# The last product of a mixer and the routing of 64 experts: other block widths, a fixed order on TensorE, and tables that move between pools

## The chip, the cores and the metric

The kernel runs on one core of one Trainium2 chip. The metric is the device time of one execution in microseconds (us); lower is better.

## What is computed

The reference runs two transformer blocks on 256 tokens of 1024 features, all in float32. The change lies at the seam between the second block's mixer and its mixture of experts:

```
merged = sigmoid(gc) * y_conv + sigmoid(ga) * y_attn
h = h + merged @ w_o                       # [256,1024] @ [1024,1024]
u = rmsnorm(h, norm2_g)
group = argmax(u @ w_group)                # 8 groups
two experts = the two highest of u @ w_router within that group (8 of 64)
y = sum over the two of weight * (silu(u @ w1[e]) * (u @ w3[e])) @ w2[e]
out = h + y
```

Each of the 64 experts has 6 MB of weights (w1, w3 of 1024 x 512, w2 of 512 x 1024), and the kernel reads all of them.

## The kernel before

**Stages.** The program runs the first block's mixer and feed-forward part, then the second block's projections, attention and convolution, then the gated merge (loop to L1052), the product with w_o (L1059 to L1086), the router (L1087 to L1205) and the expert loop (from L1290). VectorE, ScalarE, GpSimd and TensorE work on it under a scheduler that sets the order on each engine; the expert loop fixes TensorE's order by hand (`manual_schedule`).

**The product with w_o.** For full precision each weight tile is split into a high and a low part (`split`, L145 on ScalarE for the high part, L146 on VectorE for the low part), and three products are summed (`tokmm`, L269). Before the change the 1024 output columns are done in two blocks of 512. A block loads two tiles of 1 MB (L112), and each tile is split in two pieces, so there are eight pieces, 1 to 8. Each piece is used by 12 matmuls for token half t = 0 and 12 for t = 1. After a block VectorE adds the residual (L1067, result `h3`, which the program still calls xres), GpSimd writes a permuted copy `h3m` (L1070), TensorE turns h3 (L1077), ScalarE and VectorE scale it into `fT`, and TensorE forms the router's logits in `plg` (L1085).

**The router.** VectorE copies the logits to `lg` (L1088), finds the group (L1120 to L1124), masks the other groups (L1131, `rm`), takes the two best experts (L1134, L1136) and writes them as one-hot rows E1, E2 and their sum Eb in bf16 (L1142 to L1145). TensorE counts with Eb how many earlier tokens chose each expert (L1148 to L1150), VectorE makes the rank `rk` of each token (L1153, L1154) and a one-hot matrix `oh` (L1161, L1163), and TensorE gathers the tokens of four experts at a time with it (`gather`, L1171, evacuated at L1173). Then `up_mm` of expert 0 can start (L1238).

**The weights' queue.** SyncE (SP) issues the loads of expert weights, one tile of 1 MB each, in one fixed order (`load_exp`, issued at L758): tile 0, 1, 2, ... with six tiles per expert. Tile n goes to the slot that this string names, letter n modulo 21:

```
slot_order = "ggaccbbddddrrrrfeeeex"
...
p, tag, _ = slots[slot_order[n_exp[0] % len(slot_order)]]
...
with tc.issue_after(last[0]) if last else nullcontext():
    d = nc.sync.dma_start(dst, src)
```

So tiles 0 to 20 fill 21 slots, and tile 21 is the first that needs a slot again, the one of tile 0, after expert 0 has read it. `issue_after` keeps the order, and SP runs its instructions one after another: a load that waits holds up every load behind it. Tiles 0 to 4 are loaded during earlier stages. Tile 5 goes to the first buffer of pool b, tile 15 to pool f, tile 17 to a buffer of pool e.

**Where the slots lie.** The pools are laid out one after another in each partition of on-chip memory. `consts` comes first, then the ring (r), x and a, then the pools that the second block's mixer needs: `hla` (L126; eight buffers of 4096 bytes for the high and low pieces), `xpool` (L127) and others. When these are closed, the pools `small4`, `mo`, `wk4` and the slots f, b, d, e are laid into the same bytes, from where `hla` began. A tile of `pad` (L1102) lies between `wk4` and slot f:

```
pad = mo.tile([128, 80], F32, name="pad")
```

In the built program before the change `hla` ends at byte 106016 of the partition, `xpool` begins there, and so does the first buffer of pool b. A load into a slot waits until the last instruction that uses the bytes under it is done.

Of the kernel before, what the change touches and what calls it, by code (L numbers as in the profile page):

```python
# [9 lines left out]
F32 = mybir.dt.float32  # L10
# [86 lines left out]
def block_kernel(ctx: ExitStack, tc: tile.TileContext, A, out, dbg=None, stop=None):  # L97
# [7 lines left out]
    def dump(name, t):  # L105
        if name in dbg:
            nc.sync.dma_start(dbg[name], t)
# [74 lines left out]
    def cc(k):  # L182
        o, n = CLAY[k]
        return cst[:, o:o + n]
# [113 lines left out]
    def pc_(name="pc"):  # L298
        return psum.tile([128, 512], F32, name=name, tag="c", bufs=2)
# [756 lines left out]
    nc.scalar.dma_start(wr[:, :, 8:72], A["w_router_2"].rearrange("(k p) n -> p k n", p=128))  # L1056
    gain2 = pp("norm2")
    plg = pc_()
    for n in range(2):  # L1059
        pos = [pf(), pf()]  # L1060
        for pc in load_k(A["w_o_2"], n * 512, 512, "w_o"):
            for t in range(2):
                tokmm(pos[t], (mh, ml), t, [pc], first=(pc[0] == 0), last=(pc[0] == 6))
        for q in range(2):
            for t in range(2):
                c = slice(n * 512 + q * 256, n * 512 + (q + 1) * 256)
                nc.vector.tensor_add(h3[:, t, c], pos[t][:, q * 256:(q + 1) * 256], h2[:, t, c])  # L1067
        for t in range(2):
            p_ = slice(n * 64, (n + 1) * 64)
            nc.gpsimd.tensor_copy(h3m[:, t, :, p_], h3[:, t, n * 512:(n + 1) * 512].rearrange("q (p k) -> q k p", k=8))  # L1070

        for k2 in (2 * n, 2 * n + 1):
            pt = pt_()
            fT = wk.tile([128, 2, S], F32, name="fT", tag="sg", bufs=4)
            for k in range(2):
                for t in range(2):
# [5 lines left out]
            for k in range(2):  # L1082
                kt = 2 * k2 + k
                for t in range(2):
                    nc.tensor.matmul(plg[:, t * 72:(t + 1) * 72], fT[:, k, t * 128:(t + 1) * 128], wr[:, kt],  # L1085
                                     start=(kt == 0 and t == 0), stop=(kt == 7), skip_group_check=True)  # L1086
    lg = consts.tile([128, 2, 72], F32, name="lg")  # L1087
    nc.vector.tensor_copy(lg.rearrange("p t n -> p (t n)"), plg[:, :144])  # L1088
    small = consts
    rstd = rstd_of(h3, pc_(), "n4")  # L1090
    m3.close()
    dense.close()
    dump("h3", h3)
# [13 lines left out]
    def ps(name="ps"):  # L1107
        return psum.tile([128, 512], F32, name=name, tag="f", bufs=4)

    dump("lg", lg)  # L1110
    gainm = pp("norm2m")
    iota = cc("iota")
    io8 = iota[:, None, 0:8].to_broadcast([128, 2, 8])
    io64 = iota[:, None, 0:64].to_broadcast([128, 2, 64])

    gl8 = lg[:, :, 0:8]
    gm = small.tile([128, 2], F32, name="gm")
    goh = small.tile([128, 2, 8], F32, name="goh")
    gix = small.tile([128, 2], F32, name="gix")
    nc.vector.tensor_reduce(gm, gl8, axis=AX.X, op=OP.max)  # L1120
    nc.vector.tensor_tensor(goh, gl8, gm[:, :, None].to_broadcast([128, 2, 8]), op=OP.is_lt)
    nc.vector.scalar_tensor_tensor(goh, goh, 100.0, io8, op0=OP.mult, op1=OP.add)
    nc.vector.tensor_reduce(gix, goh, axis=AX.X, op=OP.min)
    nc.vector.tensor_tensor(goh, io8, gix[:, :, None].to_broadcast([128, 2, 8]), op=OP.not_equal)  # L1124
# [5 lines left out]
    for t in range(2):  # L1130
        nc.vector.scalar_tensor_tensor(rm[:, t].rearrange("p (g i) -> p g i", g=8), goh[:, t][:, :, None].to_broadcast([128, 8, 8]),  # L1131
                                       -3.0e38, lg[:, t, 8:72].rearrange("p (g i) -> p g i", g=8), op0=OP.mult, op1=OP.add)
# [9 lines left out]
    nc.vector.tensor_tensor(E1, io64, tif[:, :, 0:1].to_broadcast([128, 2, 64]), op=OP.is_equal)  # L1142
    nc.vector.tensor_tensor(E2, io64, tif[:, :, 1:2].to_broadcast([128, 2, 64]), op=OP.is_equal)
    nc.vector.tensor_add(Eb, E1, E2)
    nc.vector.tensor_add(Em, E1, E2)  # L1145

    pr = ps()
    nc.tensor.matmul(pr[:, 0:64], beforeb, Eb[:, 0], start=True, stop=True, skip_group_check=True)  # L1148
    nc.tensor.matmul(pr[:, 64:128], beforeb, Eb[:, 1], start=True, stop=False, skip_group_check=True)
    nc.tensor.matmul(pr[:, 64:128], onesb, Eb[:, 0], start=False, stop=True, skip_group_check=True)  # L1150
    rk = mo.tile([128, 2, 64], F32, name="rk")
    rk2, em2 = rk.rearrange("p t e -> p (t e)"), Em.rearrange("p t e -> p (t e)")
    nc.vector.scalar_tensor_tensor(rk2, pr[:, :128], 1.0, em2, op0=OP.add, op1=OP.mult)  # L1153
    nc.vector.tensor_scalar(rk2, rk2, -1.0, None, op0=OP.add)  # L1154
    io32 = iota[:, 0:32]

    def onehot(b4_):

# [7 lines left out]
    def gather(xg, oh, k4):  # L1166

        pg = ps()
        for k in range(4):
            for t in range(2):  # L1170
                nc.tensor.matmul(pg[:, k * 128:(k + 1) * 128], h3m[:, t, 4 * k4 + k],  # L1171
                                 oh[:, t].rearrange("p e s -> p (e s)"), start=(t == 0), stop=(t == 1))
        nc.vector.tensor_mul(xg[:, 4 * k4:4 * k4 + 4], pg.rearrange("p (k s) -> p k s", k=4),  # L1173
                             gainm[:, 4 * k4:4 * k4 + 4][:, :, None].to_broadcast([128, 4, 128]))

    by_group = {0: (wk.tile([128, 8, 128], F32, name="xg"), onehot(0))}
    gather(*by_group[0], 0)

    ge = small.tile([128, 2, 8], F32, name="ge")
    nc.vector.tensor_sub(ge, gl8, gm[:, :, None].to_broadcast([128, 2, 8]))  # L1180
# [17 lines left out]
    nc.tensor.matmul(pr[:, 128:192], onesb, Eb[:, 0], start=True, stop=False, skip_group_check=True)  # L1198
    nc.tensor.matmul(pr[:, 128:192], onesb, Eb[:, 1], start=False, stop=True, skip_group_check=True)
# [139 lines left out]
    with tc.If(most_r > SLOTS):  # L1339
# [6 lines left out]
        with tc.For_i(0, NE) as e:  # L1346
# [15 lines left out]
                                                   accum_out=dst[:, t:t + 1])  # L1362
            nc.vector.tensor_scalar(ecur, ecur, 1.0, None, op0=OP.add)
            for r in range(2):
                nc.vector.tensor_scalar(rke, rke, -float(SLOTS if r == 0 else 128), None, op0=OP.add)
# [73 lines left out]
```

## Time and profile before

| | |
|---|---|
| median of 3 runs | 1549.56 us (1547.82 to 1550.35) |
| the profiled execution's own time | 1547.5 us |
| its span, first to last instruction | 1545.7 us |
| TensorE's mean granted clock | 0.971 of full speed |
| busy: TensorE, VectorE, ScalarE, GpSimd | 88%, 39%, 27%, 8% of the span |
| read from HBM | 499.74 MB, 324 GB/s over the span |

Times in the views count from the span's start. "L758" is a line of the kernel. The 16 DMA engines are counted together: a DMA share of 1.00 means that all were moving data. Matmul ends are modelled, so neighbouring matmuls overlap in the rows, and a few matmul records can be missing.

### The profile page before, as it was taken

Reading aid. Unit: us, or ns where it says so; the run is one execution under the profiler, and the core shown is the slowest. Engines: PE = TensorE matmul, PEld = TensorE weight load, DVE = VectorE, ACT = ScalarE, POOL = GpSimd, SP = SyncE. Lnnn points to the kernel's source line nnn. Section 1 sums busy time; section 2 is a strip of 40 time slices with the busy share of each in tenths; the row PEclk is TensorE's granted clock in tenths of the full one; section 3 lists DMA queues with packets and bytes.
Section 4 is the critical chain, followed back from the end, with each engine's and each line's share of the span. In section 5 each row is a group of like instructions: output and inputs, shape, how many; then the busy total and the mean of one; then the engine's idle time right before and its main releaser. Section 6 shows DMA issues by size and latency. Waiting matters only on the chain.

```text
span 1545.7 us, 24722 instructions
## 1 busy us (share of the span) xinstructions
PE 1356.0 (88%) x10353; PEld 871.0 (56%) x10353; DVE 601.5 (39%) x1309; ACT 413.3 (27%) x734; POOL 126.8 (8%) x126
## 2 busy tenths in 40 slices
PE   7999999999999998999787888877787878878777
PEld 6766899998999996444343333333333433333332
DVE  5687777667876554322121221121111212211111
ACT  5455666555545442111000100000010100000011
POOL 3100132222111221000000000000000000000000
PEclk9999999999999999999999999999999999999999
DMA  9451656553546578999999999999999999999996
GB/s 321 131 180 56 220 190 230 176 181 107 190 140 217 190 252 341 418 419 419 419 419 419 419 419 419 419 419 419 419 419 419 419 419 419 419 419 419 419 419 243
DMA packets 137859, 502.43 MB, mean 325 GB/s; under 512 B 12545, under 2 KB 73490, under 8 KB 88722
## 3 DMA queue, kind: packets, MB, share of 16 engines
q1 hardware_dynamic: 134802, 499.67, 82.1%
q8 instruction: 83, 1.36, 0.4%
q10 hardware_dynamic: 2944, 1.16, 0.3%
q14 instruction: 30, 0.25, 0.0%
HBM read 499.74 MB, written 1.05 MB: 324 GB/s over the span
## 4 chain that ended last, share of the span: by engine, by line
DMA 56%; PE 38%; DVE 3%; SPq 1%; ACT 1%; issue 1%; POOL 0%; DVEq 0%; ACTq 0%
DMA w<-in_w 55%; PE pf L279 11%; PE pf L830 8%; PE pf L269 5%; PE acc L819 4%; PE oacc L1270 2%; PE ps L1238 2%; PE acc L269 1%; PE ps L1260 1%; PE ps L1171 1%; DMA w_go<-in_w_in 1%; DMA w_kv<-in_w_in 1%; PE pc L993 0%; PE pc L970 0%; PE pc L658 0%
## 5 line engine op out<-in xcount | busy, mean ns | idle before, releaser
L1238 PE MATMUL ps<-w,xg 128*32 128x256 f32 x4096 | 333.3, 416 | 158.8 <-DMA w<-in_w 156.4
L1238 PEld LDWEIGHTS ps<-w,xg 128*32 128x32 f32 x4096 | 145.8, 117 | 336.9 <-DMA w<-in_w 221.4
L1270 PE MATMUL oacc<-y,swT 128*128 128x512 f32 (+1 forms) x516 | 241.7, 611 | 0.6 <-DVE y L220 0.4
L1249 DVE TENSOR_TENSOR ar<-ps,a 64x128 f32<-64x128 f32 x128 | 48.9, 382 | 453.6 <-ACT a L1244 452.7
L1270 PEld LDWEIGHTS oacc<-y,swT 128*128 128x128 f32 x516 | 95.1, 195 | 128.2 <-issue 126.4
L1244 ACT ACTIVATE a<-ps 64x256 f32<-64x256 f32 x64 | 24.0, 375 | 516.0 <-PE ps L1238 516.0
L220 DVE COPY y<-ps 128x512 f32<-128x512 f32 x64 | 44.2, 691 | 218.3 <-PE ps L1260 218.3
L1260 PE MATMUL ps<-w,aT 128*32 128x512 f32 (+1 forms) x1032 | 124.5, 595 | 1.4 <-issue 1.4
L1222 ACT ACTIVATE swT<-ps 128x256 f32<-128x256 f32 x64 | 24.5, 383 | 215.7 <-PE ps L1220 215.5
L1171 PEld LDWEIGHTS ps<-oh,h3m 128*128 128x128 f32 x512 | 61.2, 196 | 26.7 <-issue 26.7
L1171 PE MATMUL ps<-oh,h3m 128*128 128x128 f32 x512 | 67.3, 286 | 1.0 <-DVE oh L1163 1.0
L218 ACT ACTIVATE y<-ps 128x512 f32<-128x512 f32 (+1 forms) x65 | 38.4, 590 | 110.1 <-PE ps L1260 110.0
L1260 PEld LDWEIGHTS ps<-w,aT 128*32 128x32 f32 x1032 | 27.4, 109 | 58.4 <-issue 46.5
L1173 DVE TENSOR_TENSOR xg<-ps,par 128x512 f32<-128x512 f32 x32 | 22.1, 691 | 69.9 <-PE ps L1171 69.9
L861 POOL TENSOR_TENSOR g<-uc,uc 128x256 f32<-128x256 f32 x22 | 31.7, 1439 | 160.1 <-ACT uc L859 151.4
L1213 DVE TENSOR_SCALAR sw<-cst,rk,Wm 128x128 f32<-128x128 f32 x128 | 38.1, 340 | 2.3 <-PE ps L1220 2.3
L1220 PEld LDWEIGHTS ps<-ident,sw 128*128 128x128 f32 x128 | 17.9, 142 | 33.9 <-issue 33.9
L146 DVE TENSOR_TENSOR w_downl<-w_down,w_downh 128x1024 fp32r<-128x1024 f32 x22 | 27.1, 1231 | 24.8 <-ACT w_downh L145 22.7
L819 PE MATMUL acc<-w_downh,gh 128*128 128x512 f32 x88 | 34.9, 397 | 0.0
L819 PE MATMUL acc<-w_downh,gl 128*128 128x512 f32 x88 | 34.8, 396 | 0.0
L819 PE MATMUL acc<-w_downl,gh 128*128 128x512 f32 x88 | 34.8, 395 | 0.0
L146 DVE TENSOR_TENSOR w_up1l<-w_up,w_up1h 128x1024 fp32r<-128x1024 f32 x22 | 26.9, 1221 | 17.1 <-ACT w_up1h L145 17.1
(532 smaller groups left out, 2179.3 us busy)
## 6 DMA issues: line engine op xcount, KB each, us to landing
w<-in_w SPq DMA_DIRECT2D x383, 1024.0 KB, 19.9
w_up<-in_w_up SPq DMA_DIRECT2D x22, 1024.0 KB, 5.2
w_down<-in_w_down SPq DMA_DIRECT2D x11, 1024.0 KB, 5.1
w_ccx<-in_w_in SPq DMA_DIRECT2D x8, 1024.0 KB, 5.0
w_g<-in_w_in SPq DMA_DIRECT2D x8, 1024.0 KB, 5.1
w_qkv<-in_w_in SPq DMA_DIRECT2D x6, 1024.0 KB, 5.1
w_out<-in_w_out SPq DMA_DIRECT2D x4, 1024.0 KB, 8.0
w_cb<-in_w_in SPq DMA_DIRECT2D x4, 1024.0 KB, 5.1
```

Source lines behind the costliest of these rows:

```text
L146: eng.tensor_sub(lo, src, hi.bitcast(F32))
L218: nc.scalar.activation(o, a, AF.Copy, scale=1.0 if scale is None else scale)
L220: nc.vector.tensor_copy(o, a)
L269: nc.tensor.matmul(o, xp[a][:, k0 + k, t * 128:(t + 1) * 128], wp[b][:, k], start=(first and j == 0 and n == 0), stop=(last and j == len(p ...
L279: nc.tensor.matmul(o, wp[b][:, k], xp[a][:, k], start=(n == 0), stop=(n == 23))
L819: nc.tensor.matmul(acc[2 * t + h], gp[a][:, t * 128:(t + 1) * 128], wd[b_][:, 0, h * 512:(h + 1) * 512], start=(ch == 0 and i == 0), stop= ...
L830: nc.tensor.matmul(pu[:, u * 256:(u + 1) * 256], cur[u][b_][:, k], hp[a][:, k], start=(kh == 0 and u == 0 and i == 0 and k == 0), stop=(i ...
L1171: nc.tensor.matmul(pg[:, k * 128:(k + 1) * 128], h3m[:, t, 4 * k4 + k], oh[:, t].rearrange("p e s -> p (e s)"), start=(t == 0), stop=(t == 1))
L1238: nc.tensor.matmul(ph[32 * g:32 * g + 32, 0:256].rearrange("p (q x) -> p q x", q=2), xg[:, 4 * k0 + k, 32 * i:32 * i + 32], w13[2 * k0 + u ...
L1249: nc.vector.tensor_mul(ar[64 * q:64 * q + 64].rearrange("p (r j) -> p j r", r=4), ph[64:128, s].rearrange("p (j r) -> p j r", r=4), a[64:1 ...
L1260: nc.tensor.matmul(py[32 * r:32 * r + 32, :n], aT[:, 32 * r:32 * r + 32], w(r), start=True, stop=True, tile_position=(0, 32 * r))
L1270: nc.tensor.matmul(oacc[2 * t + h][:, o:o + n], swT[:, t], y[:, :n], start=(e == 0), stop=(e == NE - 1), skip_group_check=True)
```

## The change

- The product with w_o is done in blocks of 512, 256 and 256 columns. The 256-column blocks load one tile of 1024 x 256 each. Pieces 5 and 6 now belong to the columns 512 to 767, pieces 7 and 8 to the columns 768 to 1023.
- TensorE's order here is written by hand: the transposes of a block stand inside the next block's second piece, before its t = 0 products, and the logits between t = 0 and t = 1. After the last block come two products of no use (`keep_busy`), the last transposes, three, the last logits, and ten; three more follow the rank products.
- VectorE no longer copies the logits (`lg` is now a view of `plg`), writes E1 and E2 in one step in bf16, no longer forms Eb, and no longer subtracts 1 from `rk` (the tables that it is compared with start at 1). The rank products read E1 and E2 in place of their sum.
- The first gather is done and evacuated in two halves.
- `gm`, `goh`, `gix`, `ge` and `rm` are now made from `consts`: the first four were in `small4`, `rm` shared a buffer in `wk4`. `lg` is gone from `consts`. `pad` is unchanged.

In bytes per partition: `consts` loses 576 (lg) and gains 512 (rm), 64 (goh), 64 (ge) and 32 each for gm and gix, in sum +128; `small4` loses 64 + 64 + 32 + 32 = 192. In the built program `hla` now ends at byte 106144, and the first buffer of pool b begins at byte 105952; slot f begins at 97760, and the `hla` buffer of the low part of piece 8 ends at 97952.

The diff, cut (the gather's halves, the exponent weights and the overflow path follow the same pattern):

```diff
-    for n in range(2):
+    PE = {mybir.EngineType.PE}
+
+    def keep_busy(n, o):
+
+        for _ in range(n):
+            nc.tensor.matmul(o.rearrange("p (r k) -> p r k", r=4), onesb, beforeb[:, None, :].to_broadcast([128, 4, 128]),
+                             start=True, stop=True, skip_group_check=True)
+
+    def block(c0, n, mids=()):
+
         pos = [pf(), pf()]
-        for pc in load_k(A["w_o_2"], n * 512, 512, "w_o"):
+        for i, pc in enumerate(load_k(A["w_o_2"], c0, n, "w_o")):
             for t in range(2):
-                tokmm(pos[t], (mh, ml), t, [pc], first=(pc[0] == 0), last=(pc[0] == 6))
+                if i == 1 and mids:
+                    mids[t]()
+                tokmm(pos[t][:, :n], (mh, ml), t, [pc], first=(pc[0] == 0), last=(pc[0] + pc[1][0].shape[1] == 8))
...
+    def turn(c0, n):
...
+    def logits(fTs):
...
+    with tc.manual_schedule(engines=PE):
+        block(0, 512)
+        fTs = []
+        for c0, n, c1, n1 in ((512, 256, 0, 512), (768, 256, 512, 256)):
+            block(c0, n, (lambda: fTs.append(turn(c1, n1)), lambda: logits(fTs[-1])))
+        idle = pf("idle")
+        keep_busy(2, idle)
+        f = turn(768, 256)
+        keep_busy(3, idle)
+        logits(f)
+        keep_busy(10, idle)
...
-    lg = consts.tile([128, 2, 72], F32, name="lg")
-    nc.vector.tensor_copy(lg.rearrange("p t n -> p (t n)"), plg[:, :144])
     small = consts
     rstd = rstd_of(h3, pc_(), "n4")
+
+    lg = plg[:, :144].rearrange("p (t n) -> p t n", t=2)
...
+    gm = small.tile([128, 2], F32, name="gm")
+    goh = small.tile([128, 2, 8], F32, name="goh")
+    gix = small.tile([128, 2], F32, name="gix")
+    rm = small.tile([128, 2, 64], F32, name="rm")
+    ge = small.tile([128, 2, 8], F32, name="ge")
...
-    gm = small.tile([128, 2], F32, name="gm")
-    goh = small.tile([128, 2, 8], F32, name="goh")
-    gix = small.tile([128, 2], F32, name="gix")
...
-    rm = wk.tile([128, 2, 64], F32, name="rm", tag="ar")
...
-    E12 = wk.tile([128, 2, 2, 64], F32, name="E12", tag="oh")
+    E12 = wk.tile([128, 2, 2, 64], BF, name="E12", tag="aT")
+    nc.vector.tensor_tensor(E12, io64, tif.rearrange("p t e -> p e t")[:, :, :, None].to_broadcast([128, 2, 2, 64]), op=OP.is_equal)
...
-    Eb = wk.tile([128, 2, 64], BF, name="Eb", tag="aT")
...
+    idle = ps("idle")
+    with tc.manual_schedule(engines=PE):
+        for i in range(2):
+            nc.tensor.matmul(pr[:, 0:128], beforeb, E12[:, i].rearrange("p t e -> p (t e)"), start=(i == 0), stop=False,
+                             skip_group_check=True)
+        for i in range(2):
+            nc.tensor.matmul(pr[:, 64:128], onesb, E12[:, i, 0], start=False, stop=(i == 1), skip_group_check=True)
+        keep_busy(3, idle)
...
-    nc.vector.tensor_scalar(rk2, rk2, -1.0, None, op0=OP.add)
-    io32 = iota[:, 0:32]
...
+    io32 = iota[:, 1:33]
...
-    gather(*by_group[0], 0)
...
+    gather(*by_group[0], 0, 2)
```

Two places of the order are needed below. The first is SP's list where the w_o tiles end and the expert tiles go on. In brackets stand the counters that an instruction waits for: DMAHW0 to DMAHW7 count landed loads, PE, DVE, Activation and Pool count finished work of TensorE, VectorE, ScalarE and GpSimd. Before the change, with tile 5 as w2_6565 and tile 6 as w1_2_6639:

```order
L112 DMA w_o_6240<-in_w_o_2 128x4x512 [waits DMAHW7_49,DVE_49]
L112 DMA w_o_6330<-in_w_o_2 128x4x512 [waits DMAHW0_49,DVE_49]
L758 DMA w2_6565<-in_w2_2 128x2048 [waits PE_49]
L112 DMA w_o_6340<-in_w_o_2 128x4x512 [waits DMAHW1_49,DVE_49]
L758 DMA w1_2_6639<-in_w1_2 128x2048
```

With the change, tile 5 is w2_6642, behind all four w_o tiles:

```order
L112 DMA w_o_6242<-in_w_o_2 128x4x512 [waits DMAHW7_49,DVE_49]
L112 DMA w_o_6308<-in_w_o_2 128x8x256 [waits DMAHW0_49,DVE_49]
L112 DMA w_o_6396<-in_w_o_2 128x8x256 [waits DMAHW1_49,DVE_49]
L758 DMA w2_6642<-in_w2_2 128x2048 [waits DVE_49,PE_49]
L758 DMA w1_2_6716<-in_w1_2 128x2048
```

Tile 5 has moved past the last w_o tile and waits for VectorE as well as for TensorE. In the built programs the counts mean this: before, TensorE's last product on w_g1l with xh (the first 8 KB of xpool); with the change, VectorE's split that writes w_ol_6311 and TensorE's last product that reads w_ol_6311, the low part of piece 5. Likewise tile 15 waited before for the last product on the low part of piece 7, and now waits for the last product on the low part of piece 8 (w_ol_6403).

The second place is TensorE's list from the end of the first 512 columns. Before (pt is a transpose, pc a logits product):

```order
L269 MATMUL pf_6229<-w_ol_6247,mh_5214 128x512 x2
L1077 MATMUL pt_6304<-ident_75,xres_67 128x128
L1077 MATMUL pt_6316<-ident_75,xres_67 128x128
L269 MATMUL pf_6328<-w_oh_6332,mh_5214 128x512 x2
L1077 MATMUL pt_6304<-ident_75,xres_67 128x128 x3
L1077 MATMUL pt_6316<-ident_75,xres_67 128x128 x3
L269 MATMUL pf_6328<-w_oh_6332,ml_5215 128x512 x2
```

With the change:

```order
L269 MATMUL pf_6231<-w_ol_6249,mh_5214 128x512 x2
L269 MATMUL pf_6306<-w_oh_6310,mh_5214 128x256 x4
L269 MATMUL pf_6306<-w_oh_6310,ml_5215 128x256 x4
L269 MATMUL pf_6306<-w_ol_6311,mh_5214 128x256 x4
L269 MATMUL pf_6307<-w_oh_6310,mh_5214 128x256 x4
L269 MATMUL pf_6307<-w_oh_6310,ml_5215 128x256 x4
L269 MATMUL pf_6307<-w_ol_6311,mh_5214 128x256 x4
L1091 MATMUL pt_6342<-ident_75,xres_67 128x128 x4
```

The 24 products of piece 5 now follow the first 512 columns directly, and the last row that names w_ol_6311 is the one that tile 5 waits for; the transposes come behind it.

## Rows read from the trace of the kernel before

**Rows 1.** The page's parts 1 and 4: the span and the chain that ended last.

```profile
span 1545.7 us, 24722 instructions
...
DMA 56%; PE 38%; DVE 3%; SPq 1%; ACT 1%; issue 1%; POOL 0%; DVEq 0%; ACTq 0%
```

**Rows 2.** Stretches: us, busy by engine, PEclk, DMA share, GB/s.

```profile
562.00:594.00 32.00, 32.00 (x199) 28.23 (x198) 15.78 (x18) 12.86 (x18) 8.52 (x7) 1.00 0.97 368
594.00:597.00 3.00, 3.00 (x15) 2.42 (x14) 0.00 (x0) 0.00 (x0) 0.00 (x0) 1.00 0.10 41
...
602.50:603.50 1.00, 0.18 (x2) 0.03 (x1) 0.78 (x7) 0.00 (x0) 0.00 (x0) 1.00 0.41 172
...
614.50:615.50 1.00, 1.00 (x11) 0.88 (x8) 0.00 (x0) 0.00 (x0) 0.00 (x0) 1.00 0.07 25
615.50:616.50 1.00, 1.00 (x11) 0.98 (x9) 0.00 (x0) 0.00 (x0) 0.00 (x0) 1.00 0.94 139
616.50:700.00 83.50, 81.36 (x738) 39.25 (x736) 23.42 (x64) 10.25 (x23) 0.00 (x0) 1.00 1.01 417
700.00:1530.00 830.00, 672.75 (x5450) 299.17 (x5450) 154.40 (x406) 75.51 (x168) 0.00 (x0) 0.95 1.01 417
```

**Rows 3.** SP's issues in order of time: start us, us, instruction; tiles 5, 6, 15, 17, 21.

```profile
562.31 0.34 SPq L758 DMA_DIRECT2D w<-in_w  x1
...
564.24 0.37 SPq L112 DMA_DIRECT2D w_o<-in_w_o  x1
564.66 0.50 SPq L758 DMA_DIRECT2D w<-in_w  x1
...
596.14 0.33 SPq L758 DMA_DIRECT2D w<-in_w  x1
...
602.75 2.03 SPq L758 DMA_DIRECT2D w<-in_w  x4
...
614.72 0.80 SPq L758 DMA_DIRECT2D w<-in_w  x2
```

**Rows 4.** The chain through 570 to 620 us: start us, us, what.

```profile
573.80 11.09 PE pf L269 x48
584.88 0.22 PE pt L1077 x2
...
598.94 0.43 DVE xres L1067
...
600.61 2.08 PE pc L1085 x16
602.69 0.02 issue
602.72 0.31 DVE lg L1088
...
607.17 0.13 DVE rk L1154
...
608.25 3.74 PE ps L1171 x16
...
612.76 1.93 PE ps L1238 x32
614.70 2.00 PE ps L1171 x16
```

**Rows 5.** The same chain earlier: 48 products of 256 columns, and eight transposes.

```profile
424.35 0.87 PE pt L985 x8
425.22 5.75 PE pf L279 x48
```

**Rows 6.** Stretches around the router: us, busy by engine, PEclk, DMA share, GB/s.

```profile
605.00:611.70 6.70, 4.05 (x21) 3.82 (x21) 4.55 (x28) 1.49 (x2) 0.00 (x0) 0.50 0.99 418
```

**Rows 7.** VectorE in order of time: a split of w_o, and the one-hot rows.

```profile
580.07 1.23 DVE L146 TENSOR_TENSOR w_ol<-w_o,w_oh 128x1024 fp32r<-128x1024 f32 x1 [1.56 <-ACT w_oh L145]
...
605.61 0.28 DVE L1143 TENSOR_TENSOR E<-cst,tif 128x128 f32<-128x128 f32 x1
```

**Rows 8.** The page's part 6: DMA issues, KB each, median us from issue to landing.

```profile
w_g<-in_w_in SPq DMA_DIRECT2D x8, 1024.0 KB, 5.1
w_qkv<-in_w_in SPq DMA_DIRECT2D x6, 1024.0 KB, 5.1
```

More of the change, by code (lines that the diff above doesn't have):

```diff
@@ L1058, in block_kernel @@
     plg = pc_()
[L1059 removed]
+    PE = {mybir.EngineType.PE}
[4 more added lines that the diff above has]
+    def block(c0, n, mids=()):
         pos = [pf(), pf()]
[L1061 removed]
+        for i, pc in enumerate(load_k(A["w_o_2"], c0, n, "w_o")):
             for t in range(2):
[L1063 to L1064 removed]
+                if i == 1 and mids:
+                    mids[t]()
+                tokmm(pos[t][:, :n], (mh, ml), t, [pc], first=(pc[0] == 0), last=(pc[0] + pc[1][0].shape[1] == 8))
+        for q in range(0, n, 256):
             for t in range(2):
[L1066 to L1067 removed]
+                c = slice(c0 + q, c0 + q + 256)
+                nc.vector.tensor_add(h3[:, t, c], pos[t][:, q:q + 256], h2[:, t, c])
         for t in range(2):
[L1069 to L1072 removed]
+            p_ = slice(c0 // 8, (c0 + n) // 8)
+            nc.gpsimd.tensor_copy(h3m[:, t, :, p_], h3[:, t, c0:c0 + n].rearrange("q (p k) -> q k p", k=8))
+    def turn(c0, n):
+        fTs = []
+        for k2 in range(c0 // 256, (c0 + n) // 256):
             pt = pt_()
             fT = wk.tile([128, 2, S], F32, name="fT", tag="sg", bufs=4)
[L1075 to L1076 removed]
+            for t in range(2):
+                for k in range(2):
                     nc.tensor.transpose(pt[:, k * 256 + t * 128:k * 256 + (t + 1) * 128],
@@ L1081, in block_kernel @@
                 copy(k, fT[:, k], pt[:, k * 256:(k + 1) * 256], scale=gain2[:, kt:kt + 1])
[L1082 to L1086, printed above, removed]
-    lg = consts.tile([128, 2, 72], F32, name="lg")
-    nc.vector.tensor_copy(lg.rearrange("p t n -> p (t n)"), plg[:, :144])
+                fTs.append((kt, fT[:, k]))
@@ new lines, in turn @@
+        return fTs
+    def logits(fTs):
+        for kt, fT in fTs:
+            for t in range(2):
+                nc.tensor.matmul(plg[:, t * 72:(t + 1) * 72], fT[:, t * 128:(t + 1) * 128], wr[:, kt],
+                                 start=(kt == 0 and t == 0), stop=(kt == 7), skip_group_check=True)
+    with tc.manual_schedule(engines=PE):
+        block(0, 512)
+        fTs = []
+        for c0, n, c1, n1 in ((512, 256, 0, 512), (768, 256, 512, 256)):
[6 more added lines that the diff above has]
+        keep_busy(10, idle)
@@ L1089, in block_kernel @@
     small = consts
     rstd = rstd_of(h3, pc_(), "n4")
+    lg = plg[:, :144].rearrange("p (t n) -> p t n", t=2)
+    iota = cc("iota")
+    io8 = iota[:, None, 0:8].to_broadcast([128, 2, 8])
+    io64 = iota[:, None, None, 0:64].to_broadcast([128, 2, 2, 64])
+    gl8 = lg[:, :, 0:8]
+    gm = small.tile([128, 2], F32, name="gm")
[3 more added lines that the diff above has]
+    ge = small.tile([128, 2, 8], F32, name="ge")
@@ new lines, in block_kernel @@
+    nc.vector.tensor_reduce(gm, gl8, axis=AX.X, op=OP.max)
+    nc.vector.tensor_tensor(goh, gl8, gm[:, :, None].to_broadcast([128, 2, 8]), op=OP.is_lt)
+    nc.vector.scalar_tensor_tensor(goh, goh, 100.0, io8, op0=OP.mult, op1=OP.add)
+    nc.vector.tensor_reduce(gix, goh, axis=AX.X, op=OP.min)
+    nc.vector.tensor_tensor(goh, io8, gix[:, :, None].to_broadcast([128, 2, 8]), op=OP.not_equal)
+    for t in range(2):
+        nc.vector.scalar_tensor_tensor(rm[:, t].rearrange("p (g i) -> p g i", g=8), goh[:, t][:, :, None].to_broadcast([128, 8, 8]),
+                                       -3.0e38, lg[:, t, 8:72].rearrange("p (g i) -> p g i", g=8), op0=OP.mult, op1=OP.add)
@@ L1091, in block_kernel @@
+    nc.vector.tensor_sub(ge, gl8, gm[:, :, None].to_broadcast([128, 2, 8]))
     m3.close()
@@ L1164, in onehot, with gather @@
         return oh
[L1166 to L1174, printed above, removed]
+    def gather(xg, oh, k4, n=4):
+        for k0 in range(4 * k4, 4 * k4 + 4, n):
+            pg = ps()
+            for k in range(n):
+                for t in range(2):
+                    nc.tensor.matmul(pg[:, k * 128:(k + 1) * 128], h3m[:, t, k0 + k],
+                                     oh[:, t].rearrange("p e s -> p (e s)"), start=(t == 0), stop=(t == 1))
+            nc.vector.tensor_mul(xg[:, k0:k0 + n], pg[:, :n * 128].rearrange("p (k s) -> p k s", k=n),
+                                 gainm[:, k0:k0 + n][:, :, None].to_broadcast([128, n, 128]))
     by_group = {0: (wk.tile([128, 8, 128], F32, name="xg"), onehot(0))}
-    gather(*by_group[0], 0)
-    ge = small.tile([128, 2, 8], F32, name="ge")
-    nc.vector.tensor_sub(ge, gl8, gm[:, :, None].to_broadcast([128, 2, 8]))
+    gather(*by_group[0], 0, 2)
     for t in range(2):
@@ L1197, in block_kernel @@
         nc.vector.scalar_tensor_tensor(Wm[:, t], E2[:, t], w2_[:, t:t + 1], Wm[:, t], op0=OP.mult, op1=OP.add)
-    nc.tensor.matmul(pr[:, 128:192], onesb, Eb[:, 0], start=True, stop=False, skip_group_check=True)
-    nc.tensor.matmul(pr[:, 128:192], onesb, Eb[:, 1], start=False, stop=True, skip_group_check=True)
+    for i in range(4):
+        nc.tensor.matmul(pr[:, 128:192], onesb, E12[:, i // 2, i % 2], start=(i == 0), stop=(i == 3), skip_group_check=True)
     most = mo.tile([128, 1], F32, name="most")
@@ L1364, in block_kernel @@
             for r in range(2):
-                nc.vector.tensor_scalar(rke, rke, -float(SLOTS if r == 0 else 128), None, op0=OP.add)
+                nc.vector.tensor_scalar(rke, rke, -float(SLOTS + 1 if r == 0 else 128), None, op0=OP.add)
                 so = wk.tile([128, 2, 128], F32, name="so", tag="oh")
```

23 lines of the change are left out of this document (2 added, 21 removed).

## The prediction

> **What bounds the kernel now.** I read the page first, then the stretches, then SP's issues, then the chain. The page says that transfers are 56% of the chain that ended last [rows 1]. The stretches say where: from 616.5 us to 1530 us the DMA share is 1.01 and the rate stays at 417 GB/s [rows 2]. For the last 900 us the kernel is a stream of 1 MB weight tiles that never stops, and TensorE, busy 672.75 of 830 us in the main stretch, keeps pace with it. One tile takes 1.0486 MB / 417 GB/s = 2.515 us. So the end is fixed by the moment from which the stream runs without a gap: every microsecond that this moment moves, the end moves.
>
> In the trace this moment is tile 21. Ahead of it the DMA engines are idle three times: at 594 to 597 (share 0.10), at 602.5 to 603.5 (0.41) and at 614.5 to 615.5 (0.07), about 2.7 + 0.6 + 0.9 = 4.2 us [rows 2]. Each gap ends with an issue by SP that had to wait: tile 15 at 596.14, tile 17 at 602.75, tile 21 at 614.72 [rows 3]. Tile 17 comes right behind the last logits (602.69), tile 21 right behind the first half of expert 0's products (612.76 + 1.93 = 614.69) [rows 4]. That is what the router's chain is worth: the gap before tile 21 is 0.9 us, and no more than the 4.2 us of all three can be won here, whatever the chain saves. A measurement of this kernel can tell about 0.2%, 3.1 us, from no change.
>
> **The layout.** This is the part of the change that its edits do not speak of, and I price it first. `consts` grows by 128 bytes and `small4` shrinks by 192, while `pad` stays. So, measured from `hla`, the slots f, b, d and e lie 192 bytes lower than before: the first buffer of pool b no longer begins where `xpool` does, but covers the last 192 bytes of `hla`'s last buffer (105952 to 106144). That buffer holds the low part of piece 5. SP's list shows the result: tile 5 now waits for VectorE too, and its counts stand for the split that writes w_ol_6311 and the last product that reads it.
>
> When is that? The first 512 columns start at 573.80 and take 11.09 us, so they end at 584.88 [rows 4]; nothing before them changes. Then come the 24 products of piece 5. 48 products of 256 columns took 5.75 us [rows 5], so 24 take 2.88: 587.76, and with a few hundredths for the release tile 5 is issued at **587.8**, where it was 562.31 [rows 3]. VectorE's split is done long before: its row starts at 580.07 and takes 1.23 us [rows 7]. The nearest other price for a product of 256 columns is the full one of 512 (11.09 / 48 = 0.231 us, 5.5 us for 24), which gives 590.4; the lower is half of it (0.116 us, 2.8 us), 587.7. I take 5.75 / 48, the same shape.
>
> SP works in order, so tiles 6 to 20, which before left from 564.66 on, stand behind tile 5. The last w_o tile still leaves at 564.24 (its wait is the same), lands some 5.1 us later [rows 8], and then the DMA engines have nothing until 588.7: a gap of 19 us under full work of TensorE. From there 16 tiles (5 to 20) need 16 x 2.515 = 40.2 us. So the stream reaches tile 21 as if it had been issued at 587.8 + 40.2 = 628.0, where it was 614.72. **The sum is +13.3 us.** It is less than the delay of tile 5, 25.5 us, because the old stream lost the difference itself: in its three gaps and by a rate of 368 GB/s at 562 to 594 [rows 2].
>
> **Does another wait come later still?** The product with w_o ends at 584.88 + 2 x 5.75 for the 256-column blocks + 0.87 + 2.08 for eight transposes and eight logits products (16 passes) + half of that again, 0.44 + 1.04, that now stand inside the blocks: 600.8, where it was 598.92 [rows 4, 5]. Tile 15, by the same shift of 192 bytes, waits for this end. The stream comes to it at 588.7 + 10 x 2.515 = 613.8, so that wait is covered, and so is tile 17's, for the last logits. They end 3.77 us after the last product before; half of the transposes and logits are gone from that stretch, so 3.77 - 0.44 - 1.04 = 2.3 us remain: 603.1, against 618.8 when tile 17's turn comes.
>
> **The router's parts,** which have to be reckoned for the rivals:
> - the copy of the logits, 0.31 us, goes, and the subtraction, 0.13 on the chain [rows 4]; three one-hot steps become one of double width, which saves between one and two of 0.28 us [rows 7]: together 0.7 to 1.0 us.
> - the idle products: the ten run while TensorE waits for VectorE anyway, the five before them cover the adds and the copies. I cost them at nothing; if their cover falls short by one product, that is 0.2 us, the price of a 512-column product.
> [...]
>
> [...] The stream reaches tile 21 only at 628.9. [...]
>
> [...]
>
> **The rivals.**
> - *A, not slower: tile 5's wait is met early,* say by an earlier user of the buffer, or the overlap does not count. It decides if tile 5 leaves before 614.72 - 40.2 = 574.5. Then tile 15 is next: 600.8 in place of 596.14, and six tiles later, 600.8 + 15.1 = 615.9, comes tile 21: +1.2 us, 1550.8. For it: before, tile 5 did not wait for w_o at all, and the overlap is 192 of 8192 bytes. Against it: the counter of VectorE is new in SP's list, and in the trace of before each of these issues follows its wait at once [rows 3, 4].
> - *B, the router decides:* both loads leave as they did, and the edits do what they add up to. Then tile 17 is the last wait, 603.1 + 4 x 2.515 = 613.2: -1.5 us, 1548.0; with all gaps gone 1545.4. For it speaks the clock at 0.50 in the gather; against it that the wait of tile 5 lies before all of it. [...]
> - *C, nothing is made up:* after the restart the stream stops again at tiles 15, 17 and 21, and the delay of 25.5 us stays whole: 1575.1. [...]
>
> **How the numbers follow.** The profiled execution took 1547.5 us with a span of 1545.7. With 13.3 us more, 1560.8 and 1559.0. The median of the runs, 1549.56, lies 2.1 us above that execution, so I expect a median of 1562.8, 0.86% more. Chances: 0.88 for this, 0.06 for A, 0.03 for B, 0.03 for C. The likely case alone spans 1560.8 less 1.3 us (the scatter of the runs) to 1565.5 (the dear price of piece 5's products) with as much above it; A, B and C hold little enough to be left outside: 1559.5 to 1566.5. Slower by over 0.2%: 0.88 + 0.03. Within 0.2%: A and most of B, 0.08. Faster: what is left of B, 0.01.
>
> **What would show it.** In the profile of the changed kernel SP should wait about 23 us, from 564.6 to 587.8, for TensorE on the w_o line; the DMA share should be near zero from some 569.5 to 588.7, and then 1.0 without a break to the end. Tile 21 should be issued by about 613 without starting a gap. The granted clock should be 1.00 through the first gather, and expert 0 should start some 2 to 3 us earlier than it did. I am wrong if tile 5 leaves before 577 us, or if the stream breaks again after 589.

## The result, and the profile after

The changed kernel takes **1559.38 us** (median of four runs, 1559.33 to 1559.99), the kernel before 1548.74 us on the same chip: ratio **1.0068**, 95% interval 1.0056 to 1.008, some 10.6 us slower. The sum had said 13.3 us. The profiled execution took 1559.99 us with a span of 1558.2 us; it starts its first expert tile 0.7 us later than the trace of before (160.54 against 159.81 us), so 0.7 us is taken off wherever the two are compared by time.

The page: the share of transfers in the chain that ended last is 62%, where it was 56% [rows 1].

```profile
span 1558.2 us, 24857 instructions
...
DMA 62%; PE 32%; DVE 3%; SPq 1%; ACT 1%; issue 0%; POOL 0%; DVEq 0%; ACTq 0%
```

What SP waited for from 560 to 640 us (total us, times, longest us):

```profile
SPq L758 <- DMA w<-in_w: 39.0, 19, 3.5
SPq L758 <- DVE w_ol L146: 13.9, 1, 13.9
SPq L758 <- PE pf L269: 10.3, 2, 9.2
```

The second row and the longest wait of the third are one wait, that of tile 5: for the split that writes the low part of piece 5, and then for the products that read it, 13.9 + 9.2 = 23.1 us (a forecast of 23). The third row's other wait, 1.1 us, is tile 15's, for the end of the product with w_o. The first row is new in this stretch: behind tile 5, SP waits 19 times for earlier loads, where before did so once here, for 0.5 us (and then 341 times from 640 to 1500 us). The chain below shows the pattern: tile 13 leaves at 593.58, and when it has landed, 21.23 us later, tile 21 follows at 614.88, eight tiles on. SP's issues (start us, us) and the chain (start us, us, what):

```profile
564.95 0.37 SPq L112 DMA_DIRECT2D w_o<-in_w_o  x1
588.47 26.74 SPq L758 DMA_DIRECT2D w<-in_w  x17
```

```profile
559.98 14.52 PE pf L279 x121
574.50 13.95 PE pf L269 x72
588.45 0.02 issue
588.47 5.05 DMA w<-in_w
...
593.58 21.23 DMA w<-in_w
...
614.88 20.07 DMA w<-in_w
```

Tile 5 leaves at 588.47 us, where before it left at 562.31 [rows 3]. It follows straight behind 72 products: 48 of the first 512 columns and the 24 of piece 5 (11.09 + 2.86 us). Less 0.7 us that is 587.8, the forecast. In before the chain ran through TensorE and the router to 616 us [rows 4]; now it turns to transfers at 588 and stays there. The stretches (us, busy by engine, PEclk, DMA share, GB/s):

```profile
569.50:588.50 19.00, 19.00 (x117) 16.91 (x116) 11.82 (x13) 7.09 (x8) 7.25 (x6) 1.00 0.01 1
588.50:589.50 1.00, 1.00 (x11) 1.00 (x10) 0.59 (x2) 0.07 (x1) 0.32 (x1) 1.00 0.21 41
589.50:600.00 10.50, 10.50 (x93) 10.50 (x92) 2.09 (x5) 3.37 (x9) 2.02 (x3) 1.00 1.00 392
600.00:603.00 3.00, 3.00 (x22) 2.05 (x20) 1.31 (x5) 1.17 (x3) 0.65 (x1) 1.00 1.01 421
605.00:612.00 7.00, 5.57 (x64) 3.63 (x61) 5.84 (x37) 1.98 (x4) 0.00 (x0) 1.00 1.02 421
616.50:700.00 83.50, 79.50 (x712) 38.80 (x705) 21.41 (x57) 9.87 (x22) 0.00 (x0) 1.00 1.01 419
700.00:1530.00 830.00, 670.01 (x5367) 296.45 (x5366) 152.09 (x400) 74.54 (x165) 0.00 (x0) 0.95 1.01 420
700.00:1500.00 800.00, 645.75 (x5184) 286.62 (x5183) 147.53 (x388) 71.83 (x159) 0.00 (x0) 0.95 1.01 420
```

Against [rows 2]: the three small gaps at 594, 602.5 and 614.5 us are gone, and one of 19 us stands in their place, with the DMA engines at 0.01. The last two rows hold a number that I had not priced, the rate: 420 GB/s. The 417 that before had up to 1530 us [rows 2] takes in the end of its stream (311 GB/s from 1515 to 1530 us), so the fair comparison is 700 to 1500 us: 420 against 419 (the row of before stands in experiment 4). In the router the granted clock is 1.00 at 605 to 612 us, where it was 0.50 [rows 6], and the rows of TensorE there show it:

```profile
603.58 2.32 PE L1064 MATMUL idle<-beforeb,onesb 128*128 128x512 bf16 x10
...
608.44 2.02 PE L1203 MATMUL ps<-oh,h3m 128*128 128x128 f32 x16 [0.54 <-DVE oh L1194]
610.39 1.93 PE L1268 MATMUL ps<-w,xg 128*32 128x256 f32 x32
```

The gather takes 2.02 us instead of 3.74 [rows 4]; expert 0 starts at 610.39 us, with the later start taken off 3.1 us earlier than before, and its first half ends at 612.3, some 2.6 us ahead of tile 21's issue at 614.88. So the router is faster as forecast, and it is worth nothing here (experiment 3 tests that).

### The profile page after: what moved, and what is told of

Read it like the earlier page. It is cut to its first block, busy times and chain, and to the rows that moved or that the text cites. A ratio compares the mean times of both kernels' runs of the same rounds, so it can differ in the third digit from the quotient of the medians.

```text
span 1558.2 us, 24857 instructions
## 1 busy us (share of the span) xinstructions
PE 1364.0 (88%) x10422; PEld 875.0 (56%) x10422; DVE 601.5 (39%) x1306; ACT 413.4 (27%) x734; POOL 127.2 (8%) x128
## 4 chain that ended last, share of the span: by engine, by line
DMA 62%; PE 32%; DVE 3%; SPq 1%; ACT 1%; issue 0%; POOL 0%; DVEq 0%; ACTq 0%
DMA w<-in_w 61%; PE pf L279 10%; PE pf L830 8%; PE pf L269 4%; PE acc L819 4%; PE acc L269 1%; DMA w_go<-in_w_in 1%; DMA w_kv<-in_w_in 1%; PE oacc L1300 0%; PE pc L993 0%; PE pc L970 0%; PE pc L658 0%; DVE tb L501 0%; PE pt L632 0%; SPq L330 0%
## 5 line engine op out<-in xcount | busy, mean ns | idle before, releaser
L1268 PE MATMUL ps<-w,xg 128*32 128x256 f32 x4096 | 337.1, 416 | 165.3 <-DMA w<-in_w 164.4
L1205 DVE TENSOR_TENSOR xg<-ps,par 128x512 f32<-128x512 f32 (+1 forms) x33 | 22.3, 675 | 67.0 <-PE ps L1203 67.0
```

The costliest lines, as they stand in the source:

```text
L1268: nc.tensor.matmul(ph[32 * g:32 * g + 32, 0:256].rearrange("p (q x) -> p q x", q=2), xg[:, 4 * k0 + k, 32 * i:32 * i + 32], w13[2 * k0 + u ...
```

## The experiments

Beside medians and ratios one number is read from each trace: the time from the landing of tile 26 to that of tile 382, 356 tiles of the unbroken stream. It repeated to 0.1 us between two profiles of one kernel (896.8 and 896.9 us before, 895.6 twice with the change), so it tells small steps that medians hide. A ratio is always to the kernel before on the same chip.

**1. The kernel before, twice, and the changed kernel again.** No edit.

> The kernel before, unchanged, as a measure of how far equal programs scatter and of how fast its stream of tiles runs in one more trace. If the missing 2.7 us of the prediction are scatter of the runs of before (S1), the ratio is 1.000 and the time from the landing of tile 26 to that of tile 382 differs from the 896.8 us of the first trace by about as much as the changed kernel's 895.6 does. If the stream really runs faster with the slots 192 bytes lower (S2), it is 896.8 again within 0.3.

> The changed kernel, unchanged, in five rounds. S1 (scatter of the few runs of before): 12 to 13 us above the kernel before in these rounds. S2 (a faster stream with the slots lower): 10 to 11 us again, and 895.6 us within 0.3 from the landing of tile 26 to that of tile 382.

Measured: before against itself 0.9997 (0.9988 to 1.0006), the changed kernel 1559.32 us, 1.0072 (1.0059 to 1.0086). The stream took 896.9 and 895.6 us again, so S2 holds: the stream of the changed kernel is 1.2 us shorter, and that is not scatter between traces. The medians lie 10.2 us apart, as S2 said. The profiled execution of before, 1549.78 us, is the slowest of its eleven runs here (the fastest took 1547.24). Its chain (start us, us, what), and TensorE's clock there, the first trace of before in the last row:

```profile
612.59 3.64 PE ps L1238 x32
616.23 2.58 PE ps L1171 x16
```

```profile
612.50:616.50 4.00, 3.91 (x33) 1.72 (x34) 0.03 (x1) 0.00 (x0) 0.00 (x0) 0.50 0.45 188
```

```profile
612.50:616.50 4.00, 3.74 (x48) 2.80 (x48) 0.21 (x1) 0.00 (x0) 0.00 (x0) 1.00 0.72 236
```

Expert 0's first half took 3.64 us at a granted clock of 0.50, where the first trace had 1.93 us [rows 4] with the clock back at 1.00. Tile 21 was issued at 616.26 instead of 614.72, and tile 26 landed 2.2 us later (635.72 against 633.48). So these two executions of before differ by 2 us (spans 1545.7 and 1547.9) through the moment at which the clock rises again after the router.

**2. The layout put right in the changed kernel; the layout alone in the kernel before.**

```diff
-    pad = mo.tile([128, 80], F32, name="pad")
+    pad = mo.tile([128, 128], F32, name="pad")     (in the changed kernel)
-    pad = mo.tile([128, 80], F32, name="pad")
+    pad = mo.tile([128, 32], F32, name="pad")      (in the kernel before)
```

> The changed kernel with pad enlarged by 48 floats (192 bytes), so that slots f and b lie again where they lay before, measured from hla; nothing else. Theory (the layout alone costs the time): tile 5 is issued at about 562 to 563 us again, the last wait that breaks the stream is tile 17's at about 603 us, and the kernel takes 1.5 us less than the kernel before (1 to 2.5 us less). Rival (the edits themselves cost the time, the 256-column blocks or the order by hand): still 10 us or more above the kernel before.

> The kernel before with pad made smaller by 48 floats (192 bytes), so that slots f, b, d and e lie as low as with the change; none of its edits. Theory (the layout alone): tile 5 waits for the last product on the low part of piece 5, which ended at about 590.3 us in the trace of before, so 590.3 + 40.2 - 614.7 = 15.8 us more by the sum of the prediction, and 13 to 16 us more if the medians fall short as they did with the change. Rival (the edits): no change within 1 us.

Measured: 1542.84 us, ratio **0.9964** (0.995 to 0.9977), and 1561.5 us, **1.0081** (1.0067 to 1.0095). The first of the two, the changed kernel with the pad of 128 floats, is called the good layout from here on. In it tile 5 leaves at 562 us again:

```profile
562.06 0.34 SPq L758 DMA_DIRECT2D w<-in_w  x1
564.00 0.37 SPq L112 DMA_DIRECT2D w_o<-in_w_o  x1
564.42 47.79 SPq L758 DMA_DIRECT2D w<-in_w  x17
```

SP's waits in the second, the old code with its slots 192 bytes lower:

```profile
SPq L758 <- DMA w<-in_w: 37.1, 18, 3.1
SPq L758 <- DVE w_ol L146: 13.9, 1, 13.9
SPq L758 <- PE pf L269: 11.9, 1, 11.9
```

and its stretch 570 to 590 us:

```profile
570.00:590.00 20.00, 20.00 (x116) 17.02 (x115) 11.89 (x15) 9.09 (x14) 7.54 (x6) 1.00 0.01 1
```

The same wait and the same hole, without one edit of the arithmetic: 192 bytes of overlap make the loss. But neither size fits. The shift alone cost 12.4 us where the sum said 15.8, and the changed kernel without it gained 5.6 us where I had 1.5. The traces say where to look. Up to the landing of tile 26 both sums hold: against the first trace of before, with the first expert tile's start taken off, the shift alone brings it 15.8 us later (649.78 against 633.48 us, less 0.5) and the good layout 1.6 us earlier (631.65, with 0.2 for an earlier start). What differs is the stream behind it: 896.8 and 896.9 us in the two profiles of before, 895.6 in both of the changed kernel, 893.9 and 894.2 here. The pace, which the prediction took as fixed, differs from program to program.

**3. Without the idle products, and another order of slots.**

```diff
-        for _ in range(n):
+        for _ in range(0):
```

```diff
-    slot_order = "ggaccbbddddrrrrfeeeex"
+    slot_order = "ggaccbbddddrrrrfexeee"
```

> The changed kernel with the pad of 128 floats and without the idle products in the router. Theory: the idle products only keep the clock up for the gather (2.02 us for its 16 products instead of 3.74 us before), and in this layout the tile that waits for expert 0's first half (issued 611.4 us with the idle products) is what the stream waits for. So it is issued 1.7 us later and the run ends 1 to 1.7 us later than with the pad alone: 1543.8 to 1544.6 us, ratio to before 0.997 to 0.9975. Rival: the load of that tile lands 7.7 us after its issue, against 5.1 us for a load that finds the engines free, so the queue is still full there and a delay of 1.7 us is hidden: 1542.8 us, the same as with the pad alone.

> The changed kernel as it is, without the idle products. Theory: the stream starts so late here (tile 5 issued 588.5 us) that the router has slack: a gather that is 1.7 us slower delays nothing, 1559.4 us, ratio 1.0065 to 1.0075. Rival: the router still sets when expert 0's buffers come free, and the run is 1.7 us longer: 1561.1 us, ratio 1.008.

> The changed kernel with the pad of 128 floats and the tile of slot x one place behind its first neighbour of slot e in the order of slots, so that the wait for h3 stands later in SP's queue. Theory: the stream still runs dry in part between tiles 15 and 17 (landings 600.9, 604.6 us, 3.7 us apart where 2.5 us is the pace), and a tile without that wait fills up to 1 us of it: 1541.8 to 1542.3 us, ratio 0.9958 to 0.9961. Rival: the tile that waits for expert 0 gates the stream at 611.4 us whatever lands before it: 1542.8 us, no change against the pad alone.

Measured: with the good layout 1544.09 us, 0.997 (0.9958 to 0.9981); in the changed kernel as it is 1559.42 us, 1.0069 (1.0055 to 1.0083); the other order 1543.82 us, 0.9965 (0.9951 to 0.9979). The stretch 605 to 612 us of the two without idle products, the good layout first:

```profile
605.00:612.00 7.00, 4.70 (x28) 4.23 (x32) 4.83 (x31) 1.98 (x4) 0.00 (x0) 0.51 0.99 407
```

```profile
605.00:612.00 7.00, 4.97 (x28) 4.29 (x32) 4.83 (x28) 1.72 (x4) 0.00 (x0) 0.54 1.02 422
```

In both the granted clock falls to about 0.5. In the changed kernel the time stays 1559.4 us: the router has slack there. With the good layout tile 21 is issued at 613.84 instead of 611.40 us (1.9 us later once the 0.5 us later start of that trace is taken off), and the median is 1.25 us higher, within the theory's range; the two intervals overlap, so the traces carry this better than the medians. The order of slots does nothing that the runs can tell.

**4. Addresses up, with no wait changed.** 128 unused bytes among the constants of the kernel before lift every buffer behind them to where the good layout has it.

```diff
     onesb = consts.tile([128, 128], BF, name="onesb")
+    shift = consts.tile([128, 32], F32, name="shift")
```

> The kernel before with 128 unused bytes among the constants: every buffer behind them lies 128 bytes higher, as in the changed kernel with the pad of 128 floats, none overlaps another than it did, and no wait changes. Theory A: the pace of the stream (tile 26 to tile 382 in 896.8 us in two profiles of before, 893.9 us in the changed kernel with the pad) hangs on the buffers' addresses: 893.9 us here, and a run of 1545 to 1546 us, ratio 0.998. Theory B: it hangs on what the engines do meanwhile (the instructions after the router, which this leaves as before): 896.8 us, 1548.7 us, ratio 0.9993 to 1.0007.

Measured: 1546.07 us, ratio 0.9979 (0.997 to 0.9988); stream 893.3 us. Theory A: 128 bytes of nothing make the old kernel 0.2% faster. That is over half of what the good layout gained beyond the forecast (5.6 against 1.5 us). Which addresses are good was open, so four more were tried, the same edit with 8, 24 and 56 floats in the changed kernel with the good layout, and with 16 in the kernel before.

> The changed kernel with the pad of 128 floats and 32 more unused bytes among the constants, so that the slots begin at multiples of 64 bytes (first buffer of b at 106176). No wait changes. Theory A: the pace hangs on whether a slot begins at a multiple of 64 bytes; then tile 26 to tile 382 takes over 1 us less or more than 893.9 us, and the two kernels with slots at multiples of 64 (this and the one with 96 bytes) agree with each other to 0.3 us. Theory B: it hangs on the address in some other way; then the value lies anywhere between the 893.3 and 896.9 us seen so far, and the run at 1542 to 1546 us (ratio 0.996 to 0.998).

> The changed kernel with the pad of 128 floats and 96 more unused bytes among the constants (first buffer of b at 106240, a multiple of 128). No wait changes. Theory A (multiples of 64 bytes decide): the same stream as with 32 bytes to 0.3 us, and over 1 us off 893.9 us. Theory B: anywhere between 893.3 and 896.9 us, a run of 1542 to 1546 us.

> The changed kernel with the pad of 128 floats and 224 more unused bytes among the constants (first buffer of b at 106368, a multiple of 128, but of no higher power of two). No wait changes. Theory A (multiples of 64 bytes decide): the same stream as with 32 and with 96 bytes to 0.3 us. Theory B: anywhere between 893.3 and 896.9 us, a run of 1542 to 1546 us.

> The kernel before with 64 unused bytes among the constants (first buffer of b at 106080, half way between 106016 with a stream of 896.8 us and 106144 with 893.3 us). No wait changes. Theory A (multiples of 64 bytes decide): the address modulo 64 is what it was in before, so 896.8 us and 1548.7 us, ratio 0.9993 to 1.0007; but the 128 bytes higher kernel has speeded up at the same remainder, which already speaks against it. Theory B: a value of its own between 893.3 and 896.9 us, a run of 1545 to 1549 us.

Measured: 1543.72 us (0.997, 0.9957 to 0.9982), **1530.01 us (0.9879, 0.9863 to 0.9895)**, 1543.89 us (0.9968, 0.9955 to 0.998) and 1545.94 us (0.9984, 0.9974 to 0.9993); streams 894.6, **882.3**, 893.6 and 893.7 us. Theory A is wrong: of three kernels with slots at multiples of 64 bytes only one is fast. That one has its slots, those of c and g excepted, at multiples of 256. Theory B named a range that was too narrow for 882. The stretch 700 to 1500 us, here and in the kernel before:

```profile
700.00:1500.00 800.00, 653.23 (x5318) 295.50 (x5310) 150.86 (x397) 73.84 (x163) 0.00 (x0) 0.96 1.01 426
```

```profile
700.00:1500.00 800.00, 649.49 (x5270) 290.02 (x5270) 149.19 (x393) 72.81 (x161) 0.00 (x0) 0.95 1.01 419
```

The DMA share is 1.01 in both; the engines are as busy and move 426 GB/s instead of 419. Tile by tile (time between neighbouring landings, grouped by the slot that the tile goes to, medians) the fast trace has 2.43 to 2.45 us for the slots r, x, a, f, b, d and e, and 2.492 us for c and g, which lie 224 bytes above a multiple of 256. In before all are at 2.485 to 2.494.

**5. Is it the remainder by 256?** All slots aligned (24 floats among the constants as above, and 56 above h3m to move c and g); the kernel before with 56 floats (remainder 0) and with 64 (the old remainder, 32); the changed kernel as it is, with its late tile 5, with 8.

```diff
     keep = ctx.enter_context(tc.tile_pool(name="keep", bufs=1, side="right", **TILE))
+    up = keep.tile([128, 56], F32, name="up")
```

> The kernel with 96 bytes among the constants (first buffer of b at 106240), and 224 unused bytes above h3m, so that the four buffers of pools c and g, the last that did not, begin at a multiple of 256 bytes too. No wait changes. In the profile with 96 bytes the tiles for c and g landed 2.492 us apart, those for the other slots 2.43 to 2.45 us. Theory: the first byte's remainder by 256 sets a tile's pace, and remainder 0 is the fast one; the 68 tiles for c and g between tile 26 and tile 382 gain some 0.05 us each, 3.4 us: stream 878.9 us, run 1526.6 us, ratio 0.9857. Rival: pools c and g are slow for another reason (their place high in memory, or the matrices that they hold): 882.3 us, 1530.0 us, as with 96 bytes alone.

> The kernel before with 224 unused bytes among the constants: first buffer of b at 106240, slots r, x, a, f, b, d and e at multiples of 256 bytes. No wait changes. Theory: the addresses alone set the pace: stream 882.3 us, 14.5 us less than the 896.8 us of before, run 1534 us, ratio 0.990 to 0.992. Rival: the fast stream needs the changed kernel's work as well: 893 to 894 us, run 1546 us, ratio 0.998.

> The changed kernel as it is (pad of 80 floats, tile 5 late) with 32 unused bytes among the constants: slots b, d, e and f begin at multiples of 256 bytes, r, x and a at a remainder of 192, c and g at 224. No wait changes, so tile 5 is issued at 587.4 to 588.5 us as in the changed kernel. Theory: the late start and the pace are two separate terms: the 186 or so tiles for b, d, e and f land 0.055 us sooner each, 10.3 us, stream 885.3 us, run 1549 us, ratio 0.999 to 1.001, though tile 5 is 25 us late. Rival: the pace needs all slots at such addresses: 893 to 896 us, run 1557 to 1560 us, ratio 1.006.

> The kernel before with 256 unused bytes among the constants: every slot lies 256 bytes higher and keeps its remainder by 256 (32 for the first buffer of b). No wait changes. Theory: only the remainder by 256 counts, so the stream takes 896.8 us as in before, and the run 1548.3 us, ratio 0.9993 to 1.0007. Rival: the address counts by another measure (the remainder by 512, or the distance to another buffer): another stream, under 895 us, and a run of under 1547 us.

Measured:

| kernel | slots r, x, a / b, d, e, f / c, g: remainder by 256 | stream, us | run, us | ratio (95% interval) |
|---|---|---|---|---|
| before | 32 / 32 / 224 | 896.8 | 1548.74 | 1 |
| before, 256 bytes up | 32 / 32 / 224 | 896.9 | 1548.28 | 1.0001 (0.9991 to 1.0011) |
| changed | 160 / 224 / 224 | 895.6 | 1559.38 | 1.0068 (1.0056 to 1.008) |
| before, 224 bytes up | 0 / 0 / 224 | 882.6 | 1534.09 | 0.9903 (0.9887 to 0.992) |
| changed, 32 bytes up | 192 / 0 / 224 | 884.6 | 1547.43 | 0.9995 (0.9986 to 1.0005) |
| good layout, 96 bytes up | 0 / 0 / 224 | 882.3 | 1530.01 | 0.9879 (0.9863 to 0.9895) |
| good layout, all slots at 0 | 0 / 0 / 0 | 881.7 | **1529.17** | 0.9878 (0.9861 to 0.9894) |

(The medians of this table come from several chips; the ratios are each to before on the same chip.) The remainder decides: 256 bytes change nothing, 224 take 14 us off the old code, and 32 bytes hide the whole loss of the change, although tile 5 still leaves at 587.51 us and the hole is still there:

```profile
570.00:587.00 17.00, 17.00 (x100) 14.92 (x99) 10.65 (x12) 7.10 (x8) 6.71 (x6) 1.00 0.01 1
616.50:700.00 83.50, 80.66 (x702) 38.35 (x702) 21.38 (x57) 9.93 (x23) 0.00 (x0) 1.00 1.01 424
700.00:1500.00 800.00, 645.61 (x5268) 291.42 (x5268) 148.75 (x391) 72.67 (x160) 0.00 (x0) 0.96 1.01 425
```

In that trace the tiles for b, d, e and f land mostly 2.43 us apart and those for r, a, c and g 2.48 to 2.49. So the late start and the pace are two terms of one sum.

The first expectation was half right. With c and g at 0 their tiles came down to 2.44 us too, yet the stream only lost 0.6 us of the 3.4 expected, and the run nothing that can be told: the tiles for b and d went from 2.43 to 2.44 us. What holds the stream at 426 GB/s then is open; no run here tells it.

## Why the prediction was right, and where it was wrong

The forecast was 1562.8 us, and 1559.38 came, just under its range: the mechanism held, and two terms of the sum were mis-sized, the step to the median and the pace.

**The layout: right.** Tile 5 waits for the products of piece 5, 587.8 us was forecast and 588.47 - 0.7 came; SP's wait of 23 us is in the rows, and so are the DMA engines that idle until about 589.3 us, 588.6 less the later start (588.7 was forecast). The w_o tiles with rows of 1 KB landed no later than forecast: the last one 4.8 us after its issue, where the sum had 5.1. The old code with the shift alone loses as much or more. That this is the cause, and not the hand-set order or the new blocks, is shown by the pair of experiment 2.

**The stream behind it: right.** It starts at 589, and from 589.5 on the DMA share is 1.00 to 1.02 in every stretch shown. Tile 15 did wait 1.1 us for the end of the product with w_o (issued at 601.00, 600.3 less the later start; 600.8 was forecast), but with earlier loads still under way, so the stream did not break. Tile 21 left at 614.88, with the later start taken off 1.2 us after the forecast 613; it came behind the landing of tile 13 and not behind the router, which was done at 612.3. Expert 0 started 3.1 us earlier, where 2 to 3 were forecast; 1.72 us of that are the gather's (2.02 in place of 3.74 [rows 4]). The router's gain lies in slack: taking the idle products out drops the clock to 0.54 and the run stays at 1559.42 us. Rivals A and C are out: tile 5 did wait, and the delay of 25.5 us did not stay whole: 13.2 us of it were left at the landing of tile 26.

**The step from one execution to the median: wrong.** "The median of the runs, 1549.56, lies 2.1 us above that execution, so I expect a median of 1562.8." The 2.1 us are no constant of the chip. The second profile of before (1549.78 us) shows where such a difference comes from: expert 0's first half at half the clock, 3.64 us in place of 1.93, and tile 21 issued 1.5 us later. My own sum had the stream at tile 21 only at 628.9, over 14 us after that tile's issue before (614.72 [rows 3]), so in the changed kernel they had to vanish, and they do: its profiled execution took 1559.99 us, and its median is not above it. The old router with the shift alone, where the stream comes late too, shows the same: its five runs lie within 0.8 us (1560.99 to 1561.75), where fifteen of before on the same chip spread over some 3 (1547.38 to 1550.43). Not all scatter comes from this place: one run of the changed kernel in experiment 1 took 1563.03 us, the ten runs with 32 bytes (experiment 5) spread over 2.6, and no run here tells why. Without the 2.1 us the same sum gives 1560.8.

**The term set to zero: the pace. Wrong.** "One tile takes 1.0486 MB / 417 GB/s = 2.515 us": the sum used this before and after. Over 356 tiles the stream was 1.2 us shorter. The spans close with it: tile 26 lands 13.9 us later (0.7 of it the later start, 13.2 the delay, where the sum had 13.3), the stream gives 1.2 back, the tail after the last landing 0.2, together 12.5 us, the difference of the spans 1558.2 and 1545.7. The forecast closes as well: 1562.8 less the 2.1, and less 0.1, 1.2 and 0.2 for these three, is 1559.2. In these runs the pace hangs on where a buffer's first byte lies by 256 (882.6 us for the old code with most slots at 0, 896.8 at 32); the change moved r, x and a from a remainder of 32 to 160 and b, d, e and f from 32 to 224. I had read the addresses for what overlaps, and not for where they begin. For the same reason the bound was wrong by which no more than the 4.2 us of the three gaps could be won: the kernel before with 224 unused bytes gained some 14 us with its waits unchanged. (One slip of arithmetic, on which nothing hangs: 1565.5 with 1.3 us above it is 1566.8, not 1566.5.)

How the pace goes with the remainder the runs show in part. 0 is the fast one: a stream of 882.6 us for the old code and 882.3 for the good layout with most slots there. There is no cost that grows with the remainder: 32 and 224 are both slow (896.8 us with most slots at 32; 2.49 us a tile at 224), while 96, 128, 160 and 192 lie a little under them (893.3 to 894.6 us). Why the remainder sets the pace, no run here shows.

**Rival B: its delay was right, and the pace was missing.** With both loads leaving as they did I had 1548.0 us, -1.5; the good layout made 1542.84, -5.6 by its ratio. Its tile 26 lands 1.6 us earlier, which is the -1.5, and its stream is 2.9 us shorter. The medians split it in much the same way: the 128 bytes higher addresses are worth 0.21% or 3.2 us (experiment 4), the idle products some 1.2 (experiment 3), which leaves about 1.2 for the other edits; the last two differences are within the intervals of the medians. In the changed kernel the router's part is hidden by tile 5.

## What to carry to other kernels

After any edit of table sizes, print where the buffers of a long stream of loads begin and what they overlap: here 192 bytes too low cost 12 us through one wait in an in-order queue, and 32 unused bytes won the same back, through the pace. Where a kernel lives on its DMA rate, try its large load targets at multiples of 256 bytes; in the good layout one unused tile of 96 bytes took 0.85% (ratios 0.9964 and 0.9879), more than all the edits of the router, and a second of 224 bytes for c and g added nothing that the runs can tell. And part of the runs' scatter belonged here to a place in the program, expert 0's first half behind the router (3.64 or 1.93 us): ask whether that place is still on the path before carrying a scatter over to the changed kernel.

## What the runs showed of the hardware that was not expected

- A stream of 1 MB loads at a DMA share of 1.01 had no fixed rate: 419 GB/s with most buffers at a remainder of 32 by 256, 426 GB/s with most at 0 (kernel before and good layout with 96 bytes, 700 to 1500 us), with the DMA engines equally busy in both. Here the share did not tell the rate.
- The effect goes tile by tile: in one and the same stream tiles for aligned slots landed 2.43 to 2.45 us apart and those for slots at 224 2.492 us.
- Two traces of the kernel before differ in the granted clock behind the router: expert 0's first 32 products took 1.93 us at 1.00 and 3.64 us at 0.50, and the spans are 1545.7 and 1547.9 us.
